# Expert stage of a two-layer encoder: slots by expert and token tile, four experts to a gather

## The chip, the cores and the metric

The program runs on one core of a Trainium2 chip. The metric is the device time of one execution in microseconds (us). Engines are named as the profile names them: PE is TensorE (PEld its weight loads), DVE is VectorE, ACT is ScalarE, POOL is GpSimd, and SP issues most of the DMAs.

## What is computed

A trunk of two encoder layers over 256 tokens of width 1024 in float32. Each layer has four token mixers, a merge, a layer norm, a feed-forward part and a second norm. Layer 0's feed-forward part is dense. Layer 1's is the stage that is changed: each token goes to two of eight experts, each of them a SwiGLU of width 1408.

```python
logits = jnp.matmul(xt, router_w).astype(F32)
top_logit, top_idx = lax.top_k(logits, TOP_K)
gates = jax.nn.softmax(top_logit, axis=-1)
...
    return jnp.matmul(jax.nn.silu(jnp.matmul(xi, w1[e])) * jnp.matmul(xi, w3[e]), w2[e])
...
y = jnp.einsum('tk,tkd->td', gates.astype(yb.dtype), yb[slot_of])
```

## The kernel before

Every float32 product is made of float32r parts. `split` makes a high part (ACT copies, named `wh`, `xh`, `hth`, `yh`) and a low part (DVE subtracts, `wl`, `xl`, `htl`, `yl`), and `mm3` multiplies high by high, high by low and low by high. Weights come by `weights`: one DMA of 512 KB into a `raw` tile, one ACT copy of 1024 columns (L211), one subtract on DVE, in a few places on POOL (L214), then six products of 512 columns. In the expert stage `raw` has 11 buffers, `wh` and `wl` five each (`ring`).

A token tile is 128 tokens on the partitions; there are two. The order of work on each engine is set by a scheduler that goes by priorities in the order of the code; each engine then runs its queue in order.

The stage goes like this. `layer_norm` centres x, `split_xT` transposes and splits it, and then, by the hook `between`, `logits` multiplies it by the router's weights (`rh`, `rl`, eight columns, stationary) for all 256 tokens at once; after that both token tiles of x get scale and bias on DVE. `route` turns the logits (`lt`) back, ranks them, and counts with a triangular matrix, over both token tiles, which slot each token has with each of its experts (`slot`). An expert has 128 slots; if some expert has more tokens, a second pass of the whole stage runs inside `If`.

`gather` takes two experts at a time. It makes a one-hot matrix `oh` (tokens by 256 slots) for each token tile on DVE, its transpose `oht` from transposed slot numbers, and multiplies x's parts (`xth`, `xtl`, stationary) by `oh`: a bank of 512 columns holds two k tiles, and each column is a sum over both token tiles, so a bank takes four products of 256 columns. ACT copies each bank (L1302) into `xh` and `xl`. The pairs of experts take the kernel's pool and the stage's pool in turn for these, so the next pair can be gathered, between the products of an odd expert, while the present one is read.

`expert_up` makes silu(x w1) * (x w3) in three column chunks, transposes it on PE (`silu`) and splits it (`hth`, `htl`). `expert_down` multiplies by w2 in two banks; `scatter` multiplies `oht` (stationary, 128 slots) by `yh` and `yl`, four banks with two products of 512 columns each, and DVE adds them, gated, to x. The products down of an expert follow the first chunk up of the next. Banks for weight products are named `mm` (four), all others `mx` (four).

## Time and profile before

| | us |
|---|---|
| three runs | 1421.01, 1428.32, 1429.54 |
| median | 1428.32 |
| span of the profiled execution, from its first to its last instruction | 1416.1 |
| runs less that span | 4.9 to 13.4 |
| PE busy in the span | 1346.5 |
| DVE busy | 1064.8 |
| ACT busy | 748.7 |

The profile's own execution is known by its span; what a run takes beyond it lies around the first and the last instruction, and differs by run. A duration of a PE instruction in the rows is modelled with its pipeline, so that a row of n products in a row is longer than what they cost; the cost is read from one row's start to the next one's.

### The profile page before, as it was taken

How to read it: one execution, taken by the hardware profiler on the slowest of the kernel's cores; microseconds unless marked ns; L12 is line 12 of the kernel's file. 1: busy time of each engine (PE TensorE's matmuls, PEld its weight loads, DVE VectorE, ACT ScalarE, POOL GpSimd, SP SyncE). 2: the span in 40 equal slices, each digit the busy share in tenths (PEclk: the TensorE clock that was granted, in tenths of full speed). 3: DMA queues.
4: the chain of work that ended last, by engine and by line, in shares of the span. 5: the costliest groups of instructions: out<-in, count | busy, mean ns of one | idle time of the engine just before them, and what ended most of it. 6: DMA issues, size and time to landing. Idle time of an engine off the chain costs nothing.

```text
span 1416.1 us, 23013 instructions
## 1 busy us (share of the span) xinstructions
PE 1346.5 (95%) x8699; PEld 1181.6 (83%) x8699; DVE 1064.8 (75%) x1843; ACT 748.7 (53%) x1086; POOL 165.4 (12%) x129
## 2 busy tenths in 40 slices
PE   8999999999699999799999999998999999999995
PEld 7878889999589998697788999986788788888874
DVE  6879865856855655788987476579888888887887
ACT  5545434444444443354544344446777777777673
POOL 1011100023300000401020002221111110210110
PEclk9999999999899999999999999998999999999998
DMA  7533421465656656554343236667989989989982
GB/s 251 166 118 95 146 75 60 135 181 179 185 177 183 190 194 193 153 150 122 106 130 95 64 102 194 181 214 262 352 301 329 335 286 359 328 309 344 326 306 88
DMA packets 155752, 281.91 MB, mean 199 GB/s; under 512 B 11120, under 2 KB 58480, under 8 KB 155632
## 3 DMA queue, kind: packets, MB, share of 16 engines
q1 hardware_dynamic: 153136, 273.54, 59.3%
q10 hardware_dynamic: 1152, 4.19, 1.0%
q0 software_dynamic: 1344, 2.62, 0.5%
q8 instruction: 70, 1.15, 0.3%
q14 instruction: 50, 0.41, 0.1%
HBM read 276.65 MB, written 2.10 MB: 197 GB/s over the span
## 4 chain that ended last, share of the span: by engine, by line
PE 84%; DVE 10%; DMA 2%; issue 2%; ACT 2%; POOL 0%; DVEq 0%; SPq 0%; ACTq 0%; POOLq 0%
PE mm L144 67%; PE mx L144 13%; PE mx L147 3%; DVE wl L214 3%; ACT wh L211 1%; DMA raw<-w_in_in 1%; DMA raw<-moe_w_in 1%; DVE x L138 1%; DVE bq L138 1%; POOL crh L754 0%; DVE cXt L130 0%; DVE rstd L138 0%; DVE cX L130 0%; PE mm L147 0%; DVE th L138 0%
## 5 line engine op out<-in xcount | busy, mean ns | idle before, releaser
L214 DVE TENSOR_TENSOR wl<-raw,wh 128x1024 fp32r<-128x1024 f32 (+3 forms) x509 | 604.4, 1208 | 188.5 <-ACT wh L211 170.9
L211 ACT CAST wh<-raw 128x1024 fp32r<-128x1024 f32 (+3 forms) x539 | 530.5, 1007 | 374.2 <-PE mm L144 309.1
L144 PE MATMUL mm<-wl,xh 128*128 128x512 f32 (+4 forms) x736 | 203.1, 368 | 3.1 <-DVE wl L214 3.1
L144 PE MATMUL mm<-wh,xh 128*128 128x512 f32 (+4 forms) x736 | 201.5, 368 | 1.1 <-ACT wh L211 0.6
L144 PE MATMUL mm<-wh,xl 128*128 128x512 f32 (+4 forms) x736 | 201.3, 366 | 0.8 <-DVE xl L190 0.8
L144 PEld LDWEIGHTS mm<-wl,xh 128*128 128x128 f32 x736 | 130.2, 190 | 22.8 <-DVE wl L214 5.1
L144 PEld LDWEIGHTS mm<-wh,xh 128*128 128x128 f32 x736 | 130.6, 191 | 20.8 <-ACT wh L211 1.4
L144 PE MATMUL mm<-xh,wh 128*128 128x256 f32 x960 | 140.9, 286 | 6.8 <-ACT wh L211 6.8
L144 PEld LDWEIGHTS mm<-wh,xl 128*128 128x128 f32 x736 | 129.6, 190 | 20.3 <-DVE xl L190 2.5
L214 POOL TENSOR_TENSOR wl<-raw,wh 128x1024 fp32r<-128x1024 f32 (+1 forms) x30 | 72.5, 2420 | 575.7 <-ACT wh L211 252.3
L144 PE MATMUL mm<-xl,wh 128*128 128x256 f32 x960 | 137.8, 284 | 0.0
L144 PE MATMUL mm<-xh,wl 128*128 128x256 f32 x960 | 137.1, 282 | 0.0
L144 PEld LDWEIGHTS mm<-xh,wh 128*128 128x128 f32 x960 | 124.8, 191 | 7.9 <-ACT wh L211 6.8
L144 PEld LDWEIGHTS mm<-xl,wh 128*128 128x128 f32 x960 | 124.2, 192 | 0.2
L144 PEld LDWEIGHTS mm<-xh,wl 128*128 128x128 f32 x960 | 122.7, 189 | 0.3
L945 POOL TENSOR_TENSOR mg<-mg,th 128x512 f32<-128x512 f32 x24 | 45.9, 1944 | 359.4 <-DVE th L138 359.4
L144 PE MATMUL mm<-wh,hth 128*128 128x512 f32 x176 | 56.1, 397 | 0.0
L144 PE MATMUL mm<-wl,hth 128*128 128x512 f32 x176 | 55.8, 396 | 0.0
L144 PE MATMUL mm<-wh,htl 128*128 128x512 f32 x176 | 55.4, 395 | 0.0
L144 PE MATMUL mm<-yT,wh 128*128 128x256 f32 x320 | 44.0, 285 | 0.0
L144 PEld LDWEIGHTS mm<-yT,wh 128*128 128x128 f32 x320 | 40.2, 191 | 0.1
L144 PEld LDWEIGHTS mm<-wh,htl 128*128 128x128 f32 x176 | 33.1, 188 | 7.7
(366 smaller groups left out, 1717.0 us busy)
## 6 DMA issues: line engine op xcount, KB each, us to landing
raw<-moe_w_in SPq DMA_DIRECT2D x215, 512.0 KB, 5.6
raw<-w_in_in SPq DMA_DIRECT2D x132, 512.0 KB, 3.8
raw<-ffn_w_in SPq DMA_DIRECT2D x66, 512.0 KB, 3.8
raw<-moe_w_in SPq DMA_DIRECT2D x64, 384.0 KB, 4.3
raw<-w_out_in SPq DMA_DIRECT2D x16, 512.0 KB, 3.5
raw<-w_branch_d_in SPq DMA_DIRECT2D x8, 512.0 KB, 3.3
raw<-w_in_in SPq DMA_DIRECT2D x8, 396.0 KB, 3.9
raw<-w_branch_b_in SPq DMA_DIRECT2D x4, 512.0 KB, 3.8
```

The source lines that it names most:

```text
L138: return self.nc.vector.scalar_tensor_tensor(o, x, s, y, op0, op1)
L144: return self.nc.tensor.matmul(o, l, r, start=start, stop=stop, skip_group_check=True)
L147: return self.nc.tensor.transpose(o, x, self.c["ident"][:x.shape[0], :x.shape[0]] if ident is None else ident)
L211: self.nc.scalar.copy(h[:, :m * n], raw[:, :m * n])
L214: eng.tensor_sub(l[:, :m * n], raw[:, :m * n], h[:, :m * n])
L945: self.nc.gpsimd.tensor_tensor(m, m, x, OP.add)
```

## The change

- An expert's 128 slots are now 64 for each token tile (`HB`). Slot numbers are counted in each token tile by itself (two products instead of five), and the second pass runs if some expert has more than 64 tokens of one tile.
- `gather` takes four experts at once. Each slot has tokens of one tile only, so nothing is summed over the tiles: the 512 columns of a bank are one k tile for four experts, and the two token tiles write 256 columns each, as four blocks of 64 with a step between them. `oh` is one comparison of 256 columns for each tile; `oht` is `oh` itself, transposed on PE and copied by DVE.
- There is one set of `xh` and `xl` for four experts, in both pools, instead of two sets in turn. In the first gather the low parts are copied by DVE, all else by ACT. The second gather (experts 4 to 7) is written between the parts of expert 3's products down, which now follow expert 3's last chunk up.
- `scatter` uses half of the rows of the array for each token tile: 64 slots, one product for tile 0 on one half and one for tile 1 on the other, each in its own bank.
- The router's x parts are the stationary operand, the weights (16 columns, high and low side by side) move; `logits` runs for each token tile as its rows come, and no transposes follow.

In the new names, `xh` and `xl` of the first pool both hold high parts (k tiles 0 to 3 and 4 to 7), and those of the second pool the low parts. Comments and docstrings, which the change also drops, are left out here.

```diff
@@ -21,6 +21,7 @@
 DEPTH = 2
 DFF = 2816
 NE = 8
+HB = 64
 DFE = 1408
 ALPHA = (2 * DEPTH) ** 0.25
 NEG = -1e30
...
@@ -994,14 +995,15 @@
             self.rsqrt_col(y[:], q[:], u[:])
             if not centred:
                 scale(t)
+            else:
+                between(t)
         if centred:
-            between()
             for t in range(2):
                 scale(t)
 
...
@@ -1171,41 +1173,44 @@
 
     def router(self, l):
         nc, gp = self.nc, self.gp
         raw, ww = (gp.tile([P, KT, NE], F32, name=n) for n in ("rw", "rww"))
         wb = gp.tile([P, 2, KT], F32, name="rwb")
         nc.sync.dma_start(raw[:], self.a["moe_router"][l // 2].rearrange("(k p) e -> p k e", p=P))
         nc.sync.dma_start(wb[:], self.a["ln1_wb"][l])
         self.tt(ww[:], raw[:], wb[:, 0][:, :, None].to_broadcast([P, KT, NE]), OP.mult)
-        self.rh, self.rl = (gp.tile([P, KT, NE], F32R, name=n) for n in ("rh", "rl"))
-        self.split(self.rh[:], self.rl[:], ww[:])
+        self.rhl = gp.tile([P, KT, 2 * NE], F32R, name="rhl")
+        self.split(self.rhl[:, :, 0:NE], self.rhl[:, :, NE:], ww[:])
         o = self.bmx()
         for k in range(KT):
             self.mm(o[:, :NE], wb[:, 1, k:k + 1].to_broadcast([P, P]), raw[:, k], k == 0, k == KT - 1)
         self.rc = gp.tile([P, NE], F32, name="rc")
         nc.vector.tensor_copy(self.rc[:], o[:, :NE])
 
-    def logits(self):
-        self.lbank = o = self.bmx()
-        self.mm3([(o[:NE, :T], (self.rh[:, k], self.rl[:, k]), self.xk(k), k == 0, k == KT - 1) for k in range(KT)])
+    def logits(self, t):
+        if t == 0:
+            self.lbank = self.bmx()
+        o = self.lbank[:, t * 2 * NE:(t + 1) * 2 * NE]
+        for k in range(KT):
+            self.mm(o, self.xh[:, k, t * P:(t + 1) * P], self.rhl[:, k], k == 0, False)
+        for k in range(KT):
+            self.mm(o[:, 0:NE], self.xl[:, k, t * P:(t + 1) * P], self.rhl[:, k, 0:NE], False, k == KT - 1)
 
     def route(self, fp):
         nc, c, o = self.nc, self.c, self.lbank
-        lt = fp.tile([NE, T], F32, name="lt")
-        nc.scalar.copy(lt[:], o[:NE, :T])
-        o = self.bmx()
-        for t in range(2):
-            self.tr(o[:, t * NE:(t + 1) * NE], lt[:, t * P:(t + 1) * P])
         sh = [P, 2, NE]
         new = lambda n, dt=F32: fp.tile(sh, dt, name=n)
         lg = new("lg")
         for t in range(2):
-            self.stt(lg[:, t], o[:, t * NE:(t + 1) * NE], self.rstd[t][:], self.rc[:], OP.mult, OP.add)
+            for i in range(2):
+                self.stt(lg[:, t], o[:, (2 * t + i) * NE:(2 * t + i + 1) * NE], self.rstd[t][:], lg[:, t] if i else self.rc[:], OP.mult, OP.add)
         gt, eq = (fp.tile([P, 2, NE, NE], F32, name=n) for n in ("gt", "eq"))
         rk = new("rk")
         full = [P, NE, NE]
...
@@ -1223,23 +1228,21 @@
         nc.vector.tensor_copy(selb[:], sel[:])
         self.lg, self.firsts = lg, (s1, s2)
         o = self.bmx()
-        self.mm(o[:, 0:8], c["ltb"], selb[:, 0])
-        self.mm(o[:, 8:16], c["ltb"], selb[:, 1], True, False)
-        self.mm(o[:, 8:16], c["onesb"], selb[:, 0], False, True)
-        self.mm(o[:, 16:24], c["onesb"], selb[:, 0], True, False)
-        self.mm(o[:, 16:24], c["onesb"], selb[:, 1], False, True)
+        sb = selb[:].rearrange("p t e -> p (t e)")
+        self.mm(o[:, 0:16], c["ltb"], sb)
+        self.mm(o[:, 16:32], c["onesb"], sb)
         self.slot = []
         for b in range(2):
             s = new(f"slot{b}")
             self.stt(s[:], o[:, :16].rearrange("p (t e) -> p t e", t=2), 1.0, sel[:], OP.add, OP.mult)
-            self.ts(s[:], s[:], -1.0 - P * b, op0=OP.add)
+            self.ts(s[:], s[:], -1.0 - HB * b, op0=OP.add)
             self.slot.append(s)
         mx, self.fullest = fp.tile([P, 1], F32, name="mx"), fp.tile([P, 1], I32, name="fullest")
-        nc.vector.tensor_reduce(mx[:], o[:, 16:24], AX.X, OP.max)
+        nc.vector.tensor_reduce(mx[:], o[:, 16:32], AX.X, OP.max)
         nc.vector.tensor_copy(self.fullest[:], mx[:])
 
         sh = [P, 2, NE]
         new = lambda n: fp.tile(sh, F32, name=n)
...
@@ -1269,44 +1272,54 @@
         return pool.tile([P, 1024], dt, name=name, bufs=b)
 
     def gather(self, l, e0, blk):
         nc, c, fp = self.nc, self.c, self.fp
         slot = self.slot[blk]
-        oh = fp.tile([P, 2, T], F32R, name="oh", bufs=2)
-        oht = fp.tile([P, 2, T], F32R, name="oht", bufs=2)
+        oh = fp.tile([P, 2, 4, HB], F32R, name="oh")
+        oht = fp.tile([P, 2, 2, P], F32R, name="oht", bufs=2)
+        sh = [P, 2, 2, HB]
         for t in range(2):
-            for i in range(2):
-                ins = self.ts(oh[:, t, i * P:(i + 1) * P], c["iota"], slot[:, t, e0 + i:e0 + i + 1], op0=OP.is_equal)
+            sl = slot[:, t, e0:e0 + 4].rearrange("p (r b) -> p r b", b=2)
+            sl = sl[:, :, ::-1] if t else sl
+            ins = self.tt(oh[:, t].rearrange("p (r b) s -> p r b s", b=2), c["iota"][:, None, None, 0:HB].to_broadcast(sh),
+                          sl[:, :, :, None].to_broadcast(sh), OP.is_equal)
         if e0 == 0 and blk == 0:
             self.hold = [ins, HOLD]
             with self.tc.issue_after(ins.ins):
                 for t in range(2):
                     self.nc.vector.tensor_sub(self.xt[1][:, t], self.x[:, t], self.xt[0][:, t])
-        for i in range(2):
-            o = self.bmx()
+        o = self.bmx()
+        for r in range(2):
             for t in range(2):
-                self.tr(o[:, t * P:(t + 1) * P], slot[:, t, e0 + i:e0 + i + 1].to_broadcast([P, P]))
-            self.ts(oht[:, i], o[:, :T], c["iotap"], op0=OP.is_equal)
-        pool = self.gp if e0 % 4 == 0 else fp
-        xg = [pool.tile([P, KT, T], F32R, name=n) for n in ("xh", "xl")]
+                self.tr(o[:, (2 * r + t) * P:(2 * r + t + 1) * P], oh[:, t, 2 * r:2 * r + 2].rearrange("p b s -> p (b s)").bitcast(F32))
+        nc.vector.tensor_copy(oht[:].rearrange("p r t s -> p (r t s)"), o[:])
+        xg = [[pool.tile([P, KT // 2, 4 * P], F32R, name=n) for n in ("xh", "xl")] for pool in (self.gp, fp)]
         yield oht, xg
-        steps = [(k0, q) for k0 in range(0, KT, 2) for q in range(2)]
+        steps = [(k, q) for k in range(KT) for q in range(2)]
         if e0 == 0:
             steps.sort(key=lambda x: x[1])
-        for n, (k0, q) in enumerate(steps):
+        for k, q in steps:
             o = self.bmx()
-            for k in range(2):
-                for t in range(2):
-                    self.mm(o[:, k * T:(k + 1) * T], self.xt[q][:, t, (k0 + k) * P:(k0 + k + 1) * P], oh[:, t], t == 0, t == 1)
-            nc.scalar.copy(xg[q][:, k0:k0 + 2, :], o[:].rearrange("p (k s) -> p k s", s=T))
-            if n % 2:
-                yield
+            ov = o[:].rearrange("p (r h s) -> p r h s", r=2, h=4)
+            for t in range(2):
+                self.mm(ov[:, :, 2:0:-1] if t else ov[:, :, 0::3], self.xt[q][:, t, k * P:(k + 1) * P],
+                        oh[:, t].rearrange("p (r b) s -> p r b s", r=2), t == 0, True)
+            dst = xg[q][k // 4][:, k % 4]
+            if e0 == 0 and q:
+                nc.vector.tensor_copy(dst, o[:])
+            else:
+                nc.scalar.copy(dst, o[:])
+            yield
 
     def expert_up(self, l, e, c0, xg, ht):
         n = min(512, DFE - c0)
-        i = slice((e % 2) * P, (e % 2 + 1) * P)
+        i = slice((e % 4) * P, (e % 4 + 1) * P)
+        xs = [[xg[q][k // 4][:, k % 4, i] for q in range(2)] for k in range(KT)]
         banks = []
         for w in ("moe_w1", "moe_w3"):
             src = self.a[w][l // 2, e][:, c0:c0 + n]
...
@@ -1314,7 +1327,7 @@
             for k in range(0, KT, 2):
                 self.pool_lo = int((w[-1], k) in UPS)
                 ws = self.weights(src[k * P:(k + 2) * P], 2, n, self.ring)
-                self.mm3([(o[:, :n], (xg[0][:, k + j, i], xg[1][:, k + j, i]), b, k + j == 0, k + j == KT - 1) for j, b in enumerate(ws)])
+                self.mm3([(o[:, :n], xs[k + j], b, k + j == 0, k + j == KT - 1) for j, b in enumerate(ws)])
             banks.append(o)
         s = self.fp.tile([P, 512], F32, name="silu", bufs=2)
         self.act(s[:, :n], banks[0][:, :n], AF.Silu)
...
@@ -1336,58 +1349,66 @@
             ws = self.weights(self.a["moe_w2"][l // 2, e][k * P:min(k + step, nf) * P, c0:c0 + n], min(step, nf - k), n, self.ring)
             self.mm3([(o[:], (ht[0][:, k + j], ht[1][:, k + j]), [q[:, i * 512:(i + 1) * 512] for q in w], k + j == 0, k + j == nf - 1)
                       for j, w in enumerate(ws) for i, o in enumerate(banks)])
+            yield
         for half, o in zip(halves, banks):
             c = slice(half * 512, (half + 1) * 512)
             self.split(y[0][:, c], y[1][:, c], o[:])
 
     def scatter(self, e, oht, y, halves):
-        for t in range(2):
-            for half in halves:
-                c = slice(half * 512, (half + 1) * 512)
-                o = self.bmx()
-                for n in range(2):
-                    self.mm(o[:], oht[:, e % 2, t * P:(t + 1) * P], y[n][:, c], n == 0, n == 1)
+        r, b = e % 4 // 2, e % 2
+        for half in halves:
+            c = slice(half * 512, (half + 1) * 512)
+            banks = [self.bmx() for _ in range(2)]
+            for n in range(2):
+                for t in range(2):
+                    s = slice(HB * (t ^ b), HB * (t ^ b) + HB)
+                    self.mm(banks[t][:], oht[s, r, t, :], y[n][s, c], n == 0, n == 1)
+            for t in range(2):
                 xv = self.x[:, t, c]
-                self.stt(xv, o[:], self.gates[:, t, e:e + 1], xv, OP.mult, OP.add)
+                self.stt(xv, banks[t][:], self.gates[:, t, e:e + 1], xv, OP.mult, OP.add)
 
     def experts(self, l, blk):
         fp, nf = self.fp, DFE // P
         ready = {}
 
         def down(e):
             oht, ht, y = ready.pop(e)
             for halves in ((0,), (1,)) if e == NE - 1 else ((0, 1),):
-                self.expert_down(l, e, ht, y, halves)
+                yield from self.expert_down(l, e, ht, y, halves)
                 self.scatter(e, oht, y, halves)
 
+        def finish(gen):
+            for _ in gen:
+                pass
         nxt = self.gather(l, 0, blk)
-        part = next(nxt)
-        for _ in nxt:
-            pass
+        oht, xg = next(nxt)
+        finish(nxt)
         if blk == 0:
             self.softmax(fp)
             for t in range(2):
                 self.ts(self.x[:, t], self.x[:, t], ALPHA)
         for e in range(NE):
-            if e % 2 == 0:
-                oht, xg = part
             y = [fp.tile([P, D], F32R, name=n) for n in ("yh", "yl")]
             ht = [fp.tile([P, nf, P], F32R, name=n, bufs=2) for n in ("hth", "htl")]
             ready[e] = (oht, ht, y)
             for c0 in range(0, DFE, 512):
                 self.expert_up(l, e, c0, xg, ht)
-                if c0 == 0 and e:
-                    down(e - 1)
-                if e % 2 and e + 1 < NE:
-                    if c0 == 0:
-                        nxt = self.gather(l, e + 1, blk)
-                        part = next(nxt)
-                    else:
-                        next(nxt)
-                        next(nxt)
-        down(NE - 1)
+                if c0 == 0 and e % 4:
+                    finish(down(e - 1))
+            if e % 4 == 3:
+                out = down(e)
+                if e + 1 < NE:
+                    nxt = self.gather(l, e + 1, blk)
+                    oht, xg = next(nxt)
+                    next(nxt)
+                    next(nxt)
+                    for _ in nxt:
+                        next(out, None)
+                finish(out)
 
     def moe(self, l):
         nc = self.nc
...
@@ -1403,7 +1424,7 @@
             self.experts(l, 0)
             self.norm_out(l, fp, *rows)
             n = nc.values_load(self.fullest[0:1, 0:1], min_val=0, max_val=T)
-            with self.tc.If(n > P):
+            with self.tc.If(n > HB):
                 self.experts(l, 1)
                 self.norm_out(l, fp, *rows)
 
```

On PE, at the scatter of expert 0 (`mx` are its banks, `mm_11073` and `mm_11072` a bank of expert 1's products up), before:

```order
L144 MATMUL mx_11041<-yh_10464,oht_10379 128x512
L144 MATMUL mm_11073<-wh_11088,xh_10394 128x512
L144 MATMUL mx_11045<-yh_10464,oht_10379 128x512
L144 MATMUL mx_11049<-yh_10464,oht_10379 128x512
L144 MATMUL mx_11053<-yh_10464,oht_10379 128x512
L144 MATMUL mm_11073<-wh_11088,xh_10394 128x512
L144 MATMUL mx_11041<-yl_10465,oht_10379 128x512
L144 MATMUL mx_11049<-yl_10465,oht_10379 128x512
L144 MATMUL mm_11073<-wh_11088,xl_10395 128x512
```

and now:

```order
L145 MATMUL mx_11056<-yh_10479,oht_10380 128x512
L145 MATMUL mx_11057<-yh_10479,oht_10380 128x512
L145 MATMUL mx_11064<-yh_10479,oht_10380 128x512
L145 MATMUL mx_11065<-yh_10479,oht_10380 128x512
L145 MATMUL mm_11072<-wh_11087,xh_10391 128x512 x2
L145 MATMUL mx_11056<-yl_10480,oht_10380 128x512
L145 MATMUL mx_11057<-yl_10480,oht_10380 128x512
L145 MATMUL mm_11072<-wh_11087,xh_10393 128x512
L145 MATMUL mx_11064<-yl_10480,oht_10380 128x512
L145 MATMUL mx_11065<-yl_10480,oht_10380 128x512
```

There are eight scatter products as before; the two of a pair (banks 11056 and 11057, 11064 and 11065) now stand side by side, and products of the full array stand between three groups of them. Over the eight experts there are 21 such groups: three in expert 0, two in expert 1, three in expert 2, one in expert 3, and three in each of the others.

On DVE, where the first gather is made (`xtl` is x's low part, `p`, `g` and `gate` belong to the gates, `wl` to expert 0's weights), before:

```order
L1284 TENSOR_TENSOR xtl<-x,xth 128x1024 x2
L134 TENSOR_SCALAR oht<-mx,c_160 128x256 x2
L130 TENSOR_TENSOR p_10451<-l_10446,l_10445 128x2
L134 TENSOR_SCALAR x<-x 128x1024 x2
L214 TENSOR_TENSOR wl<-raw,wh 128x1024
L134 TENSOR_SCALAR oh<-c_160,slot_10360 128x128
```

and now:

```order
L1292 TENSOR_TENSOR xtl<-x,xth 128x1024 x2
L1298 CAST oht<-mx 128x512
L131 TENSOR_TENSOR p_10466<-l_10461,l_10460 128x2
L135 TENSOR_SCALAR x<-x 128x1024 x2
L215 TENSOR_TENSOR wl<-raw,wh 128x1024
L1313 CAST xh<-mx 128x512 x4
L1313 CAST xl<-mx 128x512 x4
L135 TENSOR_SCALAR g_10467<-p_10466 128x2
L215 TENSOR_TENSOR wl<-raw,wh 128x1024
```

Eight copies of 512 columns stand between the first and the second `wl` of the stage, where one-hot matrices of the next pairs of experts stood.

## Rows read from the trace of the kernel before

**Rows 1.** The page, its head and busy time by engine.

```profile
span 1416.1 us, 23013 instructions
PE 1346.5 (95%) x8699; PEld 1181.6 (83%) x8699; DVE 1064.8 (75%) x1843; ACT 748.7 (53%) x1086; POOL 165.4 (12%) x129
```

**Rows 2.** Windows: length, busy PE, PEld, DVE, ACT, POOL; clock, DMA share, GB/s.

```profile
953.80:978.30 24.50, 16.23 (x89) 12.45 (x88) 22.93 (x76) 11.73 (x19) 3.90 (x2) 0.72 0.78 276
978.30:1397.90 419.60, 408.64 (x1936) 339.55 (x1934) 358.99 (x372) 307.66 (x368) 55.63 (x23) 1.00 0.88 313
```

**Rows 3.** Waits from 978.3 to 1397.9, of PE and of ACT: total, times, longest.

```profile
PE mx L147 <- DVE silu L130: 5.7, 7, 1.2
ACT wh L211 <- PE mm L144: 39.2, 98, 2.4
```

**Rows 4.** Gather: the tile oh's products, and PE's timeline: start, length, count.

```profile
L144 PE MATMUL mx<-oh,xth x64: 277/283/582, 971.7 to 1279.7; 128*128 128x256 f32 x64
...
1173.61 0.64 PE L144 MATMUL mx<-oh,xtl 128*128 128x256 f32 x4
1174.09 0.64 PE L144 MATMUL mx<-oh,xth 128*128 128x256 f32 x4
```

**Rows 5.** PE's timeline: four transposes, and the product after them.

```profile
992.30 0.66 PE L147 MATMUL mx<-c,silu 128*128 128x128 f32 x4 [1.14 <-DVE silu L130]
992.71 0.48 PE L144 MATMUL mm<-wh,xl 128*128 128x512 f32 x1
```

**Rows 6.** Scatter: the tile oht's products, and PE's timeline.

```profile
L144 PE MATMUL mx<-yh,oht x32: 387/397/504, 1041.0 to 1399.0; 128*128 128x512 f32 x32
...
1390.79 0.62 PE L144 MATMUL mx<-yh,oht 128*128 128x512 f32 x2
1391.25 0.40 PE L144 MATMUL mm<-wh,hth 128*128 128x512 f32 x1
```

**Rows 7.** PE's timeline in layer 0: products on half of the array's rows (64*128).

```profile
87.60 1.16 PE L144 MATMUL mx<-csl 64*128 64x128 f32 x16
88.69 0.73 PE L144 MATMUL mx<-crh,cafter 128*128 128x512 f32 x2
89.27 0.39 PE L144 MATMUL mx<-c 128*128 128x512 bf16 x1
...
94.83 0.61 PE L144 MATMUL mm<-wh,xl 128*128 128x512 f32 x2
95.38 1.49 PE L144 MATMUL mx<-csl 64*128 64x128 f32 x16
```

**Rows 8.** Timelines of PE, DVE and ACT, from the router to the first weight products.

```profile
961.64 1.87 PE L144 MATMUL mx<-xh,rh 128*8 128x256 f32 x8 [1.31 <-DVE xl L190]
...
971.70 3.18 PE L144 MATMUL mx<-oh,xth 128*128 128x256 f32 x12
...
978.27 0.63 PE L144 MATMUL mm<-wh,xl 128*128 128x512 f32 x2
...
960.81 2.47 DVE L190 TENSOR_TENSOR xl<-mx,xh 128x512 fp32r<-128x512 f32 x4
...
965.73 1.28 DVE L972 TENSOR_TENSOR x<-x,lnb 128x512 f32<-128x512 f32 x2
967.39 0.36 DVE L138 SCALAR_TENSOR_TENSOR lg<-mx,rstd,rc 128x8 f32<-128x8 f32 x2 [0.38 <-PE mx L147]
...
976.05 1.22 DVE L214 TENSOR_TENSOR wl<-raw,wh 128x1024 fp32r<-128x1024 f32 x1
...
980.48 5.75 DVE L214 TENSOR_TENSOR wl<-raw,wh 128x1024 fp32r<-128x1024 f32 x5
...
977.04 2.06 ACT L1302 CAST xl<-mx 128x512 fp32r<-128x512 f32 x4 [0.26 <-PE mx L144]
...
979.06 1.07 ACT L211 CAST wh<-raw 128x1024 fp32r<-128x1024 f32 x1
```

**Rows 9.** SP's timeline: issues of the experts' weights before and after x is gathered.

```profile
959.63 5.54 SPq L206 DMA_DIRECT2D raw<-moe_w_in  x5
977.29 11.39 SPq L206 DMA_DIRECT2D raw<-moe_w_in  x7
```

## The prediction

> **What bounds the kernel now.** I read the page's head first: PE is busy for 95% of a span of 1416.1 us [rows 1]. Then the windows cut that span at the stage that changes [rows 2]. The long window, 419.6 us of the eight experts' products, has PE busy for 408.6 us at the full clock, DVE for 359.0, ACT for 307.7, and the DMA engines at 0.88. The third view is the waits of that window [rows 3]: ACT's largest is 39.2 us for PE, that is for `wh` buffers that PE has not yet read, so the weights come early enough; PE's largest is 5.7 us in all, for the product of silu. So PE's own work sets the stage's time. A product less is worth its own length, as long as DVE, at 86% of the window, keeps up. The short window before it (953.8 to 978.3) is otherwise: PE is busy for 16.2 of 24.5 us at a mean clock of 0.72, DVE for 22.9; there a DVE instruction counts and a PE product mostly does not. Nothing ahead of the router's products moves on any engine, so layer 0 and the mixers keep their times.
>
> **Gather, on the path.** Before, each of four pairs of experts takes 32 products of 256 columns, 128 in all (64 with `xth`, and as many with `xtl`) [rows 4]. Now each of two fours takes 16 banks of two products, 64 in all. Four of them take 1174.09 - 1173.61 = 0.48 us, 0.12 each [rows 4], so 64 fewer are worth -7.7 us. No product in the trace writes a bank in blocks with steps between them, as the new ones do. The nearest row is the same count of columns in one piece, 0.12; the far end is a price for each block of 64 as for a product of its own, some 0.10 to 0.11 as a transposed block of 128 has [rows 5], 0.33 us more for each of 64, +21 us. I take 0.12, since the columns are what the rows follow: 0.12 for 256 here and 0.23 for 512 in the scatter. The one-hot transposes go from 16 to 8, at 0.41 / 4 = 0.10 us [rows 5]: -0.8 us.
>
> **Scatter, on the path.** 64 products of 512 columns before (32 with `yh`, 32 with `yl`), 0.46 / 2 = 0.23 us each, 14.7 us [rows 6]. Now there are 64 products on half of the rows each, two of which can run at once. That they do is seen in layer 0: 16 products on half arrays take 88.69 - 87.60 = 1.09 us [rows 7], where eight of 128 columns on the full array take 8 x 0.10 = 0.82 [rows 5] and sixteen 1.64. So 32 pairs cost 7.4 us: -7.4. But the same rows show a price for going to half arrays and back. The entry: two products from 94.83 would end at 95.29, and the half arrays start at 95.38, 0.09. Inside: 1.09 against 0.82, 0.27. The way back: the two products of 512 columns behind take 89.27 - 88.69 = 0.58 in place of 0.46, 0.12 [rows 7]. That is 0.48 a visit, or 0.40 if a pair takes 0.11; I take 0.44. The scheduler lays the scatters out in 21 visits, since products of the next expert stand between the groups: 21 x 0.44 = +9.2 us. The scatter then costs 1.8 us more than before. Its ends are -7.4 (the price is hidden behind the products around it) and +9.2 (the price stays and the two of a pair do not overlap).
>
> The Trainium skill, in "TensorEngine Tiling (Array Packing)", section "Key Properties", says that a change of the tiling mode drains the engine, and in its "Overview" promises a factor of up to two for a contraction of 64 or less. Layer 0's rows show both. By the factor alone the sum below would be lower by the 9.2 us of the visits.
>
> **The router and the first gather, DVE's path.** The 24 router products start at 961.64 and stand, with a copy and two transposes, ahead of `lg` at 967.39; but DVE is at work on x until 965.73 + 1.28 = 967.01 anyway [rows 8], and keeps that order. So the shorter router is worth only 0.38 us. Two more operations on `lg` (0.36 for two [rows 8]) and three fewer tiny products for the slots about cancel. I take -0.4; the ends are -1 and +0.5.
>
> Then the low parts of the first gather move from ACT (four banks in 979.06 - 977.04 = 2.02 us, about 0.5 each) to DVE, behind the `wl` at 976.05. Eight copies of the size of an `xl` subtract (2.47 / 4 = 0.62 [rows 8]) run from 977.3 to 982.2. The gather has four banks, so its last products wait for the fourth copy, 979.7; PE has eight weight products between them. Before, PE had done two such products by 978.27 and then one each 0.23 us, nine by 979.9 [rows 8]. So PE is where it was: 0. The next `wl` follows at 983.4 instead of about 981.6 (980.48 + 5.75 / 5); PE comes to it some 26 products after 978.27, at 984.3, so that about 1 us of slack is left where 2.7 were. I take 0, and +2 as the upper end, which also stands for a clock that stays at half for longer, since PE waits between the copies (972 to 976 is at half speed already, as the 12 products from 971.70 show with 0.26 each [rows 8]).
>
> SP now waits for the count of the fullest cell between its twelfth and thirteenth early weight load instead of at the end. It issues nothing between 965.17 and 977.29 before, for lack of `raw` buffers [rows 9], and the count is ready ahead of the gather at 971.7. So the wait costs nothing; without that pause all weights behind it would be late by as much.
>
> **The second gather, ACT's path.** There is one set of `xh` and `xl`, so the 16 copies for experts 4 to 7 start only when expert 3's products up are done, and stand among 11 `wh` copies of its products down: 16 x 0.52 + 11 x 1.05 + the copies of `yh` and `hth` (1.5) = 21.4 us of ACT [rows 8], beside 66 x 0.23 + 32 x 0.12 = 19.0 us of PE. ACT falls behind by 2.4 us, and up to five `wh` tiles (1.4 us of PE each) lie ready. I take +1; the ends are 0 and 8.3, all 16 copies exposed. Before, the same copies lay in two groups with a set of buffers of their own, and the pairs' gathers gave ACT and DVE time to catch up.
>
> **The end.** The last scatter's four products run as two pairs, -0.2 us.
>
> **The sum** is -7.7 - 0.8 + 1.8 - 0.4 + 0 + 1.0 - 0.2 = -6.3 us, a span of 1409.8. What lies around the span (4.9 to 13.4 us by run) is untouched, so I take the same 6.3 us off the median: 1428.32 - 6.3 = 1422.0 us, -0.4%. About 1%, 14.3 us, is what a measurement here can tell from no change, with runs that differ by 8.5 us.
>
> **The rivals.**
>
> *The visits are free.* If the weights of a half-array product load while full-array products run, the 9.2 us go, and the sum is -15.5: 1412.8 us. Against it speak layer 0's rows, each of which shows the price; for it, that those are float32 products between others of their kind, and that PE's stalls for silu leave some place to hide in.
>
> *Four experts' copies are exposed* (the slower side). The copies sit between the gather's products and the first product up that reads them. It decides from the point at which PE's next product up needs a part that is not yet copied, and no `wh` is left that it can use before. Then the second gather costs 8.3 us instead of 1 and the first one 8 x 0.62 = 5.0 instead of 0: -6.3 + 7.3 + 5.0 = +6.0, 1434.3 us. For it: one set of buffers, ACT 2.4 us short, DVE's slack down to 1 us. Against it: products down, which need none of these parts, lie between, and expert 4's first products ask for k tiles in the order of the copies.
>
> *The stepped writes are dearer.* At twice the price of contiguous ones the gather's gain is gone, +7.7: 1429.7; at the far end, +21, it is 1443. No row speaks for it.
>
> *The second pass runs.* It would add a stage, over 400 us. The reference's own inputs put at most 41 of a tile's 128 tokens with one expert, below 64, so it doesn't.
>
> **How the numbers follow.** The forecast has 0.60, free visits 0.16, exposed copies 0.12, dearer writes 0.10 (0.03 of it at the far end), anything else 0.02. The likeliest is the forecast, 1422. The range runs from the free visits' 1412.8 less 2 to the exposed copies' less 2, 1411 to 1432; outside it lie part of the last two rivals. Faster by over 1% (under 1414.0) is most of the free visits and a little of the forecast, 0.16. Slower by over 1% (over 1442.6) is the far end of the writes and what is left, 0.05. Within 1% is 0.79.
>
> **What would show it.** Right: 64 gather products at 0.12 us in the long window, which gets 5 to 8 us shorter while its DVE time stays within 2 us of 359; scatter pairs that start a few ns apart with 0.3 us in place of 0.23 to the next full product; `lg` at 967.0; weight products without a pause from about 980. Wrong: gaps of PE of several us before products that read the gathered parts, at the start or at expert 4; gather products spaced at 0.2 us or more; half-array products one after the other; or a scatter whose neighbours keep their 0.23 us.

## The result, and the profile after

The changed kernel takes 1412.53 us (median of 20 runs, 1405.2 to 1427.24) beside 1420.09 of the kernel before (20 runs, 1413.75 to 1431.03), a ratio of 0.9945 with a 95% interval of 0.9919 to 0.9971: 4.1 to 11.5 us less. The forecast was 6.3 us less, within 1%. It was taken off the median of three runs of the kernel before, 1428.32, and so put the changed kernel at 1422.0 us; 8.2 of the 9.5 us by which it came out below that are the base, whose median over 20 runs is 1420.09. Runs of either kernel differ with TensorE's mean clock: the changed kernel took 1405.2 us at 0.979 and 1427.24 at 0.960. The experiments show that the sum of -6.3 us came out for other reasons than the prediction gave, and in part by luck.

The page's head and busy times of the profile after, beside [rows 1]:

```profile
span 1411.3 us, 22852 instructions
PE 1345.2 (95%) x8630; PEld 1175.9 (83%) x8630; DVE 1065.4 (75%) x1835; ACT 741.5 (53%) x1077; POOL 169.9 (12%) x129
```

The 4.8 us between the spans are not the change's worth: of these two profiles only this one has PE at half clock (1.2 GHz) from 730 to 740 us (last section). So I compare from the start of the last product with w_out on, in three windows: to the gather, to the last product down, and to the end. In the kernels with the old gather the second window starts at the first product of `oh` with x, in those with the new one at the first transpose of `oh`, 0.1 to 0.2 us ahead of that product. Columns as in [rows 2]. Before:

```profile
953.98:971.70 17.72, 9.45 (x54) 6.06 (x52) 16.99 (x67) 7.25 (x11) 3.90 (x2) 0.75 0.93 329
971.70:1397.63 425.93, 414.97 (x1969) 345.80 (x1968) 364.49 (x382) 312.11 (x375) 55.63 (x23) 0.99 0.87 311
1397.63:1416.10 18.47, 1.85 (x6) 0.59 (x4) 11.60 (x35) 3.14 (x5) 1.70 (x1) 0.65 0.17 62
```

After:

```profile
957.44:975.77 18.33, 10.65 (x52) 9.42 (x51) 17.18 (x66) 8.13 (x11) 3.90 (x2) 0.63 0.93 333
975.77:1392.93 417.16, 408.26 (x1899) 332.43 (x1900) 363.97 (x374) 304.02 (x366) 59.60 (x23) 1.00 0.88 317
1392.93:1411.30 18.37, 1.39 (x6) 0.37 (x4) 11.62 (x35) 3.14 (x5) 1.64 (x1) 0.58 0.17 62
```

The first window is 0.6 us longer, the long one 8.8 shorter, the end 0.1 shorter: 462.1 us become 453.9, 8.2 less, inside the interval. All windows here come from one profile of each kernel. PE's waits in the long window, of the kind in [rows 3] (before: 5.7 for silu, 3.1 for wl, the first line):

```profile
PE mm L144 <- DVE wl L214: 3.1, 4, 1.0
PE mm L145 <- DVE wl L215: 4.0, 4, 1.0
PE mx L148 <- DVE silu L131: 3.6, 4, 1.2
```

The gather, beside [rows 4]: the tile's products, and a piece of PE's timeline.

```profile
L145 PE MATMUL mx<-oh,xth x32: 274/282/582, 975.9 to 1192.2; 128*128 128x256 f32 x32
...
979.63 0.87 PE L145 MATMUL mx<-oh,xth 128*128 128x256 f32 x6
980.34 2.12 PE L145 MATMUL mx<-oh,xtl 128*128 128x256 f32 x10
```

Half of the products are left, and (980.34 - 979.63) / 6 = 0.12 us each: blocks of 64 with steps cost no more than a piece.

The scatter, beside [rows 6]: PE's timeline at expert 0's.

```profile
1045.16 0.62 PE L145 MATMUL mm<-wl,xh 128*128 128x512 f32 x2
1045.71 0.83 PE L145 MATMUL mx<-yh,oht 64*128 64x512 f32 x4
1046.47 0.73 PE L145 MATMUL mm<-wh,xh 128*128 128x512 f32 x2
1047.63 0.50 PE L145 MATMUL mx<-yl,oht 64*128 64x512 f32 x2 [0.42 <-DVE yl L191]
1048.06 0.49 PE L145 MATMUL mm<-wh,xh 128*128 128x512 f32 x1
1048.48 0.49 PE L145 MATMUL mx<-yl,oht 64*128 64x512 f32 x2
1048.90 0.50 PE L145 MATMUL mm<-wh,xh 128*128 128x512 f32 x1
```

A pair's two products do start together (3 ns apart), and the price of a visit is there: a product on the full array after a pair, and a pair after such a product, each start 0.42 us after the one before (0.43 and 0.42 from 1047.63 on), where two full ones are 0.23 apart. A four of products takes 0.76 to the next full one, not 0.46.

The router, beside [rows 8]: PE's timeline,

```profile
962.28 1.02 PE L145 MATMUL mx<-rhl,xh 128*128 128x16 f32 x4 [0.43 <-ACT xh L190]
963.16 0.90 PE L148 MATMUL mx<-c,x 128*128 128x128 f32 x3
963.71 1.00 PE L145 MATMUL mx<-rhl,xh 128*128 128x16 f32 x4
...
965.88 1.11 PE L148 MATMUL mx<-c,x 128*128 128x128 f32 x4
```

and ACT's:

```profile
965.08 0.59 ACT L190 CAST xh<-mx 128x512 fp32r<-128x512 f32 x1 [2.36 <-PE mx L148]
967.03 0.59 ACT L190 CAST xh<-mx 128x512 fp32r<-128x512 f32 x1 [1.37 <-PE mx L148]
```

Tile 0's products, 0.22 us each for 16 columns (four from 962.28 to 963.16), stand between the transposes of tile 1, and ACT waits 2.36 and 1.37 us for these. The granted clock is 0.50 for all of the router's products. `lg` starts 13.95 us after the last product with w_out where it was 13.41 (967.39 - 953.98).

### The profile page after: what moved, and what is told of

It is laid out like the page before. It is cut to its first block, busy times and chain, and to the rows that moved or that the text cites. A ratio compares the mean times of both kernels' runs of the same rounds, so it can differ in the third digit from the quotient of the medians.

```text
span 1411.3 us, 22852 instructions
## 1 busy us (share of the span) xinstructions
PE 1345.2 (95%) x8630; PEld 1175.9 (83%) x8630; DVE 1065.4 (75%) x1835; ACT 741.5 (53%) x1077; POOL 169.9 (12%) x129
## 3 DMA queue, kind: packets, MB, share of 16 engines
q1 hardware_dynamic: 153136, 273.54, 57.4%
q8 instruction: 70, 1.15, 0.3%
## 5 line engine op out<-in xcount | busy, mean ns | idle before, releaser
L145 PE MATMUL mm<-wh,xh 128*128 128x512 f32 (+4 forms) x736 | 191.1, 371 | 1.1 <-ACT wh L212 0.8
L145 PE MATMUL mm<-wh,xl 128*128 128x512 f32 (+4 forms) x736 | 185.1, 367 | 0.8 <-DVE xl L191 0.8
L145 PE MATMUL mm<-wl,xh 128*128 128x512 f32 (+4 forms) x544 | 148.7, 368 | 4.0 <-DVE wl L215 4.0
L215 POOL TENSOR_TENSOR wl<-raw,wh 128x1024 fp32r<-128x1024 f32 (+1 forms) x30 | 76.5, 2553 | 562.2 <-ACT wh L212 290.2
L145 PEld LDWEIGHTS mm<-wl,xh 128*128 128x128 f32 x544 | 95.3, 192 | 19.9 <-DVE wl L215 6.0
L145 PE MATMUL mm<-wl,xl 128*128 128x512 f32 (+1 forms) x192 | 56.6, 376 | 0.0
L145 PEld LDWEIGHTS mm<-wl,xl 128*128 128x128 f32 x192 | 35.7, 188 | 6.0 <-DVE wl L215 0.5
```

The costliest lines, as they stand in the source:

```text
L145: return self.nc.tensor.matmul(o, l, r, start=start, stop=stop, skip_group_check=True)
L215: eng.tensor_sub(l[:, :m * n], raw[:, :m * n], h[:, :m * n])
```

## Why PE waits for silu

One of the four waits for silu in the kernel after, in the timelines of POOL,

```profile
1003.48 2.69 POOL L215 TENSOR_TENSOR wl<-raw,wh 128x768 fp32r<-128x768 f32 x1 [7.67 <-ACT wh L212]
```

DVE,

```profile
1004.75 2.23 DVE L215 TENSOR_TENSOR wl<-raw,wh 128x768 fp32r<-128x768 f32 x1 [0.31 <-ACT wh L212]
1006.90 0.68 DVE L131 TENSOR_TENSOR silu<-silu,mm 128x512 f32<-128x512 f32 x1
1007.50 0.95 DVE L215 TENSOR_TENSOR wl<-raw,wh 128x768 fp32r<-128x768 f32 x1
```

and PE:

```profile
1007.64 0.66 PE L148 MATMUL mx<-c,silu 128*128 128x128 f32 x4 [1.06 <-DVE silu L131]
```

In each of the 24 passes of products up (23 records) POOL makes one `wl`. A `wl` on DVE that starts beside it ends about 0.8 us behind POOL's end (1006.98 against 1006.17), 2.23 us in all, where the next takes 0.95. DVE's product of silu is queued behind it, and PE, whose queue has silu's transposes next, stands for 1.06 us. Both kernels have POOL's `wl` in the same passes, and in neither has PE a wait of over 0.15 us for POOL's own `wl`.

This is no single case. In the two traces 38 of DVE's `wl` start while POOL makes one. Of these, 35 end 1.08 to 1.09 us (1024 columns) or 0.81 to 0.85 us (768 columns) behind POOL's end, whenever they started; in the other three places it is POOL's own that is long (3.10, 3.28 and 3.87 us). All seven waits for silu before and all four after stand behind such a longer `wl` (1.35 to 2.70 us). Beside 1.22 and 0.95 us alone, DVE's are longer by some 15 us in all in either kernel, so the kernels differ in which instruction stands behind them.

The Trainium skill, "SBUF — State Buffer", section "Who interferes with whom", says that a DVE instruction with two SBUF inputs contends with a GpSimd instruction that reads SBUF, and that the port pair they share is an exclusive lock. These rows agree: however early it starts, a `wl` of DVE with 768 columns ends some 0.8 us behind POOL's, and alone it takes 0.95.

## The experiments

All kernels in one table: the ratio to the kernel before, the first two windows as above, and PE's waits in the second for silu and for `wl` of DVE, by the profile. The last window is 18.3 to 18.7 us in all. The first window repeats within 0.02 us in the kernels that leave the router and POOL alone; how well the long one repeats is not known.

| kernel | ratio, 95% interval | to the gather | long window | silu | wl |
|---|---|---|---|---|---|
| before | 1 | 17.72 | 425.93 | 5.7 | 3.1 |
| after | 0.9945 (0.9919 to 0.9971) | 18.33 | 417.16 | 3.6 | 4.0 |
| 1 gather twice | 1.0005 (0.9978 to 1.0033) | 18.33 | 427.75 | 6.9 | 3.9 |
| 2 pairs on half arrays | 1.0341 (1.0282 to 1.0399) | 18.34 | 474.51 | 10.4 | 0 |
| 3 products on the full array | 1.0079 (1.0053 to 1.0105) | 18.34 | 437.12 | 9.6 | 0 |
| 4 yl first | 0.9895 (0.9858 to 0.9932) | 18.33 | 413.15 | 4.0 | 1.2 |
| 5 scatter on the full array | 0.9889 (0.9825 to 0.9952) | 18.34 | 417.06 | 1.6 | 5.2 |
| 6 router of before | 0.9920 (0.9877 to 0.9963) | 16.96 | 417.75 | 1.6 | 4.9 |
| 7 copies on ACT | 0.9950 (0.9908 to 0.9992) | 18.34 | 418.80 | 4.2 | 4.9 |
| 8 POOL's wl half a pass later | 0.9961 (0.9926 to 0.9996) | 19.02 | 420.30 | 0 | 10.4 |
| 9 after, no wl on POOL | 0.9892 (0.9839 to 0.9946) | 19.66 | 410.93 | 0 | 3.1 |
| 10 as 4 and 6 | 0.9903 (0.9865 to 0.9940) | 16.95 | 416.00 | 3.5 | 2.6 |
| 11 as 4, 6 and 9 | 0.9899 (0.9849 to 0.9949) | 16.96 | 408.46 | 0 | 4.7 |
| 12 before, no wl on POOL | 0.9905 (0.9870 to 0.9940) | 17.30 | 413.96 | 0 | 2.0 |

**1. The gather's products twice.**

```diff
-            for t in range(2):
-                self.mm(ov[...], self.xt[q][...], oh[:, t]..., t == 0, True)
+            for _ in range(2):
+                for t in range(2):
+                    self.mm(ov[...], self.xt[q][...], oh[:, t]..., t == 0, True)
```

> The changed kernel with each of its 64 gather products issued twice into the same bank; the second issue writes the same values. Nothing else is changed. My theory (a gather product is on the path, with its own length of 0.12 us): the stretch from the last product with w_out to the end, 453.9 us in the changed kernel's profile, gets 64 x 0.12 = 7.7 us longer, 461.6, and the whole comes back to the kernel before within 2 us. Rival 'the copies bound the gather' (ACT and DVE, not PE, set its pace, so the count of products does not matter): under +2 us. Rival 'stepped writes are dearer': over +12 us.

The long window grew by 10.6 us. The gather's own products, each counted from its start to the next start, grew by 7.3, as expected; the other 3.3 are silu's waits (6.9 for 3.6), which the edit doesn't touch. That was the first hint that these move by themselves.

**2 and 3. The price of a visit.** For half arrays:

```diff
+        spare = [self.bmx() for _ in range(2)]
         for k in range(0, nf, step):
 ...
+            for i in range(2):
+                s = slice(HB * i, HB * i + HB)
+                self.mm(spare[i][:], self.xt[0][s, 0, 0:P], self.xt[0][s, 1, 0:512])
```

> The changed kernel with a pair of extra products on half of the rows each (64 rows, 128 x 512, into two spare banks that nobody reads) behind every k tile of the products down: 89 pairs, each between products on all 128 rows. The trace of the changed kernel puts a pair at 0.23 us and a change to half arrays and back at some 0.32 us: 89 x 0.55 = +49 us on the 453.9 us from the last product with w_out to the end. By the 0.44 us of the prediction: 89 x 0.67 = +60. If a change is free: 89 x 0.23 = +20.5. If the two of a pair do not overlap, and a change is free: +41, but then the two of a pair start 0.23 us apart.

For the full array, at the same places:

```diff
+            self.mm(spare[0][:], self.xt[0][:, 0, 0:P], self.xt[0][:, 1, 0:512])
```

> The same as the one with extra pairs on half arrays, but each pair is one product on all 128 rows (128 x 512 into one spare bank), at the same 89 places. All theories: 89 x 0.23 = +20.5 us on the 453.9 us from the last product with w_out to the end, since no change of the array's shape is added. The difference to the kernel with half arrays, divided by 89, is the price of a change there and back, if a pair takes as long as one product: 0.32 by the trace of the changed kernel, 0.44 by the prediction, 0 by the rival of free visits.

The long window grew by 57.4 and 20.0 us; the difference is 37.4 / 89 = 0.42 us a visit. It holds 0.8 us more of silu's waits and, as the scatters came to lie otherwise, 113 visits against 20; by these it is 36.6 / 93 = 0.39. PE's timeline of the first:

```profile
1035.32 0.62 PE L145 MATMUL mm<-wl,hth 128*128 128x512 f32 x2
1035.87 0.50 PE L145 MATMUL mx<-xth 64*128 64x512 f32 x2
1036.30 0.73 PE L145 MATMUL mm<-wh,hth 128*128 128x512 f32 x2
1036.87 0.63 PE L145 MATMUL mm<-wh,htl 128*128 128x512 f32 x2
```

From 1035.32 to 1036.87 four full products and a pair take 1.55 us; five full ones would take 1.15. The prediction's 0.44, taken from layer 0's small float32 products, held within 0.05; free visits are refuted.

**4. Fewer visits.** The products with yl go first; yl is ready last.

```diff
-            for n in range(2):
+            for n in (1, 0):
 ...
-                    self.mm(banks[t][:], oht[s, r, t, :], y[n][s, c], n == 0, n == 1)
+                    self.mm(banks[t][:], oht[s, r, t, :], y[n][s, c], n == 1, n == 0)
```

> The changed kernel, with the scatter's products with yl ahead of those with yh. yl is ready last, so none of the products is issued alone: the 21 visits to half arrays become about 9, with the same 64 products. At 0.32 us a visit the 453.9 us get 12 x 0.32 = 3.8 us shorter, at 0.44 us 5.3. By 'visits are free': no change (within 1 us). What speaks against it: at the end of the program two pairs stand behind the last yl where one did, +0.3 us, and a scatter that waits for yl with nothing left beside it would cost 0.4 us each time.

The visits fell from 21 to 9. The long window lost 4.0 us, the end gained 0.3. Eight products now go in one visit:

```profile
1108.04 1.07 PE L145 MATMUL mm<-wh,xh 128*128 128x512 f32 x4
1109.03 0.50 PE L145 MATMUL mx<-yl,oht 64*128 64x512 f32 x2
1109.37 0.40 PE L145 MATMUL mx<-yh,oht 64*128 64x512 f32 x2
1109.61 0.39 PE L145 MATMUL mx<-yl,oht 64*128 64x512 f32 x2
1109.84 0.40 PE L145 MATMUL mx<-yh,oht 64*128 64x512 f32 x2
1110.16 0.73 PE L145 MATMUL mm<-wl,xh 128*128 128x512 f32 x2
```

Inside this visit the second pair starts 0.34 us after the first and the next two 0.24 and 0.23 us later; four pairs cost 1.13 us to the next full product.

**5. Scatter on the full array.** It needs zeros in the other half of `oht`'s rows; the small copies and memsets that make them are left out here.

```diff
 ...
-                    self.mm(banks[t][:], oht[s, r, t, :], y[n][s, c], n == 0, n == 1)
+                    self.mm(banks[t][:], oht[:, r, b, t, :], y[n][:, c], n == 0, n == 1)
```

> The changed kernel with its scatter on all 128 rows: the transposed one-hot tile holds each expert and token tile apart, zero in the other half of the rows, so a product takes all of yh or yl, and there is no change to half arrays; 64 products one after the other. It adds six small copies on VectorE and two memsets on GpSimd. If a visit costs 0.40 to 0.42 us (the difference of the two kernels with extra products, 37.4 / 89): 64 x 0.23 - (32 x 0.23 + 21 x 0.41) = -1.2 us on the 453.9 us from the last product with w_out to the end. By the prediction's sum: -1.8. By the rival of free visits: +7.4. Where PE waits for silu, both could be covered by up to 2.6 us either way, as these waits differ by that between kernels that don't touch them (6.4 us before, 3.8 after, 7.1 with the gather twice).

The windows lost 0.1 us in all, with 2.0 less for silu, 1.2 more for DVE's `wl` and 1.6 more for `wh` (2.4 for 0.8). So half arrays with 21 visits are worth nothing here, and the 7.4 us that free visits would be worth are excluded; whether the visits cost 1 us more than the pairs save can't be told from these two kernels.

**6. The router of before.**

```diff
-            else:
-                between(t)
         if centred:
+            between()
```

with `logits`, `rh`, `rl`, `lt` and its transposes as they were.

> The changed kernel with the router of before: logits for both token tiles at once behind both normalisations, then lt, its two transposes and one operation per tile for lg. My reading of the trace after: the products of tile 0, at half clock and with a weight load of 128 columns for each 16 columns, stand between the transposes of x and delay them, so from the last product with w_out to the first gather product it is 18.33 us where it was 17.72; with the old router 17.7 again, and the whole 0.6 us shorter. By the prediction (the new router is worth 0.4 us): 18.7, and 0.4 us longer.

The first window fell to 16.96, by 1.4 us, more than either view: the new router costs 1.4. Of that 1.0 lies ahead of `lg` (12.97 us after the last product with w_out, 13.95 with the new router) and 0.4 between `lg`, now four operations instead of two, and the gather. The edit takes back the order of the products and their number together, and in every kernel with the new router the clock is at half from at most 5.8 us after the last product with w_out until the gather, which takes in nearly all of its products; so the shares of order and clock stay open.

Of the 0.8 us by which this window is shorter than before (17.72 to 16.96) only 0.2 can be the fewer slot operations: from `lg` to the first gather product it is 4.09 us, and 4.31 before. 0.4 lie ahead of `lg`, where the kernel before waits 0.38 us for PE with the router's products at half clock, and this one does not wait; kernel 12, which has nothing of the change, does not either (13.00 us to `lg`). The last 0.1 is there because the window ends at a transpose here and at the first product before. The long window took 0.6 back.

**7. The first gather's copies all on ACT.**

```diff
-            if e0 == 0 and q:
+            if False:
```

> The changed kernel with all 16 copies of the first gather on ScalarE, none on VectorE. In the changed kernel VectorE's eight copies start at 981.21, 5.4 us behind the first gather product, since the copy of oht, ALPHA times x and a wl come first, and the weight products run without a pause 6.9 to 7.1 us behind the first gather product where it was 6.1 before. Theory 'VectorE's late copies cost the 0.8 us': the stretch from the first gather product to the last product down, 417.2 us, gets 0.8 shorter. Theory 'four experts' copies cost it on either engine' (16 x 0.52 = 8.3 us of ScalarE, and the wh casts wait behind them): the same within 0.5, or longer by up to 2 us. By the prediction (the copies are free on VectorE): no gain.

1.6 us longer, of which 0.6 and 0.9 are silu's and `wl`'s waits; the 0.1 that is left says that the copies cost the same on either engine. VectorE's copies as such are not the cause of what the start lost.

**8 and 9. POOL's wl.**

```diff
-UPS, DOWNS = (('1', 4),), ()
+UPS, DOWNS = (('3', 2),), ()
```

> The changed kernel with the one wl of each pass of products up that GpSimd subtracts moved from w1's third pair of k tiles to w3's second, half a pass later. In the changed kernel four of the 24 passes have PE waiting some 1.3 us (3.8 us in all) for silu, each time just behind a wl on VectorE that takes 2.1 to 2.8 us in place of 1.2 beside GpSimd's wl. Theory 'the neighbour on GpSimd makes silu late': the waits go, -3 to -4 us on the 453.9 us. Rival 'silu's chain is late by itself' (the product, Silu on ScalarE, the product on VectorE): the waits stay, within 1 us. A third way: w3's products now wait for a wl, as much as is gained.

Silu's waits went, and 6.4 us more for `wl` came: the third way.

```diff
-UPS, DOWNS = (('1', 4),), ()
+UPS, DOWNS = (), ()
```

> The changed kernel with every wl of the products up on VectorE, none on GpSimd (the edit is to a table; no work is left out). In the changed kernel VectorE has 11 wl of 1.5 to 2.8 us beside the 24 of GpSimd, and PE waits 3.8 us for silu behind such a one and 4.0 us for wl. Theory 'the neighbour on GpSimd costs VectorE what it saves': both waits fall, -3 to -7 us on the 453.9 us. Rival 'VectorE is then too slow' (24 x 1.2 = 29 us more on an engine at 365 of 420): waits for wl grow by more than the silu waits fall, 0 to +10 us, as moving GpSimd's wl half a pass later did (+3.8, silu's waits gone, 6.4 us more for wl).

The long window lost 6.2 us. DVE's and POOL's `wl` in the kernel after (minimum, median, maximum in ns):

```profile
L215 DVE TENSOR_TENSOR wl<-raw,wh x255: 685/1219/2834, 980.1 to 1391.5; 128x1024 fp32r<-128x1024 f32 x94, 128x768 fp32r<-128x768 f32 x32, 128x512 fp32r<-128x512 f32 x2
L215 POOL TENSOR_TENSOR wl<-raw,wh x23: 1850/2519/3869, 993.3 to 1365.2; 128x1024 fp32r<-128x1024 f32 x15, 128x768 fp32r<-128x768 f32 x8
```

DVE's without POOL:

```profile
L215 DVE TENSOR_TENSOR wl<-raw,wh x278: 684/1217/1227, 979.6 to 1384.9; 128x1024 fp32r<-128x1024 f32 x107, 128x768 fp32r<-128x768 f32 x32
```

and the long window then:

```profile
975.34:1386.27 410.93, 406.97 (x1900) 332.74 (x1900) 372.33 (x397) 303.71 (x366) 0.00 (x0) 1.00 0.88 320
```

DVE has 23 more of them, some 26 us (15 of 1.22 and 8 of 0.95), yet is busy for only 8.4 us more (372.33 for 363.97): the neighbour had cost it most of what it saved. The first window is 1.3 us longer. A `wl` of DVE now stands there between the norm's operations, but it does in kernel 12 too, whose first window is 0.4 us shorter than that of the kernel before; in kernel 9 DVE waits 1.24 and 0.87 us for `xh` there, in kernel 12 it has no such wait, and kernel 11, with the old router, needs 16.96. So the loss comes with the new router.

**10 and 11. The edits together.**

> The changed kernel with the scatter's products with yl first (9 visits in place of 21; alone it gave -3.7 us on the 453.9 us) and the router of before (alone -0.8). If the two add up: 449.4 us, some 9% of it as little as 4.5 us, and a ratio of 0.991 to 0.992 to the kernel before. If the moved start of the weight products brings other waits for silu and wl, as between the kernels so far: 447 to 452.

> The same two edits and no wl of the products up on GpSimd. If GpSimd's wl costs VectorE what it saves: 3 to 7 us less than with the two edits alone, about 444 us from the last product with w_out to the end. If VectorE is then too slow: 449 to 459.

With 4 and 6 the three windows take 451.6 us, within the 447 to 452 that were expected if other waits come; with 4, 6 and 9 444.1, as expected and the least of all: 9.8 us less than the changed kernel and 18.0 less than before. Its ratio beats the kernel before; against kernels 4, 9 and 12 the times don't separate it, since those of kernel 11 alone run from 1400.4 to 1416.1 us.

**12. The kernel before without POOL's wl.** The same edit as 9, to the kernel before.

> The kernel before, with every wl of the products up on VectorE, as in the changed kernel without GpSimd's wl, whose stretch from the first gather product to the last product down takes 410.9 us. Without GpSimd neither kernel should wait for silu, and their difference is what the change itself is worth on this stretch. My theory: of the 8.8 us by which this stretch is shorter in the changed kernel, 2.4 us are waits for silu and wl that fell otherwise, and the change itself gives 8.0 - 1.0 (scatter) - 0.8 (late copies of the first gather) = 6.2 us: 417.1 us here. Rival 'the waits are part of the change's gain' (its order of the work keeps silu clear of them): the difference stays 8.8 us, 419.7 here. If neither holds and VectorE, with the pairs' one-hot operations on it, becomes too slow: above 422.

Its long window, and PE's waits in it:

```profile
975.28:1389.24 413.96, 411.34 (x1969) 345.46 (x1968) 373.43 (x405) 313.53 (x375) 0.00 (x0) 1.00 0.88 319
```

```profile
PE mm L144 <- DVE wl L214: 2.0, 3, 1.0
```

A miss for every theory, mine too: 413.96 us, 12.0 less than with POOL. Of these 0.8 come ahead of POOL's first `wl` of the long window: from the first gather product to the weight products behind the gather it is 5.73 us at a mean granted clock of 0.81, and 6.57 at 0.65 before. So some 11 us are left for POOL's `wl`.

Without `wl` on POOL the change is worth 413.96 - 410.93 = 3.0 us on the long window, not 6.2 and not 8.8. Over all three windows it is worth less still: kernel 12 takes 449.6 us and kernel 9 449.0, since kernel 9's first window is 2.4 us longer. Their ratios to the kernel before don't tell the two apart. Kernel 11, with yl first and the old router, is 5.5 us below kernel 12 by the windows.

## Why the prediction was right

The sum of -6.3 us lies within the interval and 2 us from the windows' -8.2. Two of its signs did not come: `lg` was to stand at 967.0, 13.0 us after the last product with w_out, and came after 13.95; the long window was to be 5 to 8 us shorter and is 8.8. By its own terms, with PE's products counted from start to start:

- *Gather, -7.7*: -7.4. Kernel 12 spends 17.3 us on its 128 products and kernel 9 9.9 on 64. Stepped writes cost nothing extra; that rival is gone.
- *One-hot transposes, -0.8*: +0.2 on the long window, 0.82 us for 12 in kernel 12 and 0.98 for 8 in kernel 9, four of these at half clock; the other four of before stood ahead of it.
- *Scatter, +1.8*: right in its price (0.39 to 0.42 us a visit against 0.44) and its overlap (a pair at 0.23). 21 x 0.42 - 7.4 = +1.4; between kernels 12 and 9 the scatter's own products fall by 2.1 us, and the 23 visits of kernel 9 lengthen the products around them by about 0.2 each, so some +2.
- *Router, -0.4*: wrong in its sign; `lg` came 0.54 us later and the first window is 0.6 us longer. The step that failed is that it only shortens what stands ahead of `lg`: I counted the products, not what they stand between. Tile 0's came between the transposes of tile 1, and DVE's path, which the prediction had as the limit, runs through those. Kernel 6 shows +1.4 for the new router as a whole; the fewer slot operations gave at most 0.2 back, and 0.4 are the wait that the kernel before had for its own router and kernel 12 has not.
- *First gather, 0*: from the start of the long window to expert 0's first product down 49.9 us in kernel 9 and 48.5 in kernel 12, +1.4, inside the upper +2. Some 0.6 of it are four transposes of `oh`, counted above, that now lie in it, and the clock is lower (0.60 against 0.72 over the first 4 us). Kernel 7 shows no gain from ACT.
- *Second gather, +1.0*: not seen where it was put. Its products run from 1166 to 1188 us in kernel 9, and PE has no wait of over 0.15 us between 1147 and 1248. Kernel 9 waits 1.1 us longer for `wl` than kernel 12, but in other passes. The rival of exposed copies didn't come, nor did the second pass run.
- *End, -0.2*: -0.1.

On the long window that is the 3.0 us between kernels 12 and 9, and with the first window and the end as first measured (+0.6 and -0.1) -2.5 in all. The other 5.7 us are in no term: without `wl` on POOL the kernel before gets 425.93 - 413.96 = 12.0 us shorter, 0.8 of it by the clock, and the changed one 6.2. The step that failed is the first one, "PE's own work sets the stage's time", with the waits for silu named and then held constant. They are not: 1.6 to 10.4 us for silu among the kernels that leave POOL's `wl` where it was. That the sum of -6.3 met the -8.2 is luck: the terms were some 4 us too good, and the waits gave more than that. Why the kernel before met them oftener is not settled: it depends on which instruction of DVE stands behind a `wl` beside POOL's, and so on all that stands in the queues of both.

## What to carry to other kernels

A wait of a few us that both kernels share is no constant: when an edit is worth less than the waits in the window, take the waits away in both and compare again, or the sum is right by chance. Before giving work to GpSimd, look how long VectorE's instructions beside it get, not only at what VectorE is spared. Count a change of the array's shape by visits, and put products that can go together into one.

## What was not expected

- Ten microseconds at the lower of PE's two clock levels, 1.2 GHz, among products of layer 1's mixers, with PE busy all the time in the 5 us before it fell and while it was low. The windows of the profile after:

```profile
725.00:730.00 5.00, 5.00 (x58) 4.00 (x57) 4.10 (x16) 2.28 (x8) 1.72 (x4) 1.00 0.59 168
730.00:735.00 5.00, 5.00 (x24) 4.41 (x25) 1.41 (x4) 1.97 (x4) 2.13 (x4) 0.52 0.27 100
735.00:740.00 5.00, 5.00 (x30) 4.76 (x29) 1.61 (x8) 2.25 (x5) 0.00 (x0) 0.50 0.35 107
```

  The profile before has 1.00 in all three. Kernel 8's has 0.50 from 723.4 to 747.3 us, with PE busy for 3.99 of the 5 us before. What lowers it stays open.
- 24 `wl` on POOL, meant to relieve DVE, cost the kernel before some 11 us of its long window.
